# Three matmuls of 256 columns in place of a pair, in a kernel with split float32 weights

## The chip, the core and the metric

The kernel runs on one core of a Trainium2 chip. The metric is the device time of one execution in microseconds, from the runs of the kernel alone; the profile is one further execution, recorded with every engine's instructions. The engines are called by the profile's short names: PE is TensorE (PEld its loading of weights), DVE is VectorE, ACT is ScalarE, POOL is GpSimd, SP is SyncE, whose queue issues the loads.

## The reference

One layer of a decoder trunk on 256 positions and 2048 channels, in float32:

```python
h = rms_norm(x, pre_g)
proj = h @ w_in
a_u, a_v, a_g, b_x, b_g, x_q, x_g, gate_logits = jnp.split(proj, splits, axis=-1)
y_a = spatial_gating(a_u, a_v, sg_ln_g, sg_ln_b, sg_w, sg_b) * jax.nn.silu(a_g)
y_b = s5_branch(b_x, ..., glu_w, glu_b) * jax.nn.silu(b_g)
y_x = memory_cross_attention(x_q, rms_norm(mem, mem_g), xa_wk, xa_wv) * jax.nn.silu(x_g)
branch = jnp.einsum('bsnc,ncd->bsnd', jnp.stack([y_a, y_b, y_x], axis=2), w_branch)
gates = jax.nn.sigmoid(gate_logits.reshape(bsz, seq, N_BRANCH, D_MODEL))
out = jnp.sum(gates * branch, axis=2) @ w_out
return x + rms_norm(out, post_g)
```

Each of a_u to x_g is 1024 channels wide, the gate logits 3 x 2048. The state-space branch (s5_branch) runs a complex scan over the positions for 64 groups of 16 channels, applies a GELU, and ends in a gated linear unit: y times the sigmoid of y @ glu_w + glu_b. The cross-attention has 4 heads over 256 memory tokens.

## The kernel before

**Split numbers.** Every large product is made of numbers split in two: the high part is the value rounded to the matmul's reduced format (float32r), the low part is the rest. A product is then high by high, high by low and low by high. The weights come from memory as float32 in pieces of 128 x 2048 (`load`), and each half piece is split by `split` (lines 86 to 94): ScalarE makes the high part (line 93), VectorE subtracts to get the low part (line 94), into one of three buffers of the tag "hl". The activations are split once: x into the 16 tiles `xhl`, the memory tokens into `mhl`, the state-space output into `ygl`.

**Two kinds of product.** In the time-major kind (`tm_mm`, lines 181 to 184) the activations are the loaded operand and the weights move, 512 columns at a time. The change doesn't touch it. In the channel-major kind the weights are loaded, 128 x 128 at a time, and the activations move: the result has 128 channels in the partitions and 256 positions (T) in the columns. Its step, for one block of 128 inputs, is `cm_mm` (lines 169 to 174): a pair of matmuls. One has the high weights and moves 512 columns, high and low activations side by side, into a result of two halves of 256 columns; the other has the low weights, moves the 256 high columns, and adds to the first half. The two halves are then added, which gives the three products. In every step but the first of a block the matmul with the low weights comes first (line 171); in the first it comes second (line 174). `cm_mm3` (lines 176 to 179) does the same in three matmuls of 256 columns into the first half alone; only wk uses it.

**Adding the halves.** `fold` (lines 230 to 234) copies the second half out of the accumulator with ScalarE (line 232) and adds the first half with VectorE (line 233) into a tile of the tag "w0". `fold_u` (lines 338 to 340) does the same into its destination, for u and for the queries. After `fold` come: a multiplication by `rx2`, the row of inverse norms (line 327), then a SiLU for w_ag and w_bg (`silu`, lines 692 to 696); the multiplication alone for w_xg (`evac_xg`, line 755) and w_au (line 874); a sigmoid with bias for the GLU (line 908).

**Order.** `cm_block` runs a block of 16 steps, 8 for each half piece; `cm_pairs` runs two blocks into one accumulator of two banks (of which there are two), then calls the function that takes the result out. The stages that matter here, in order: the first four blocks of w_bx together with the splitting of x; four more blocks of w_bx; w_xq (8 blocks); wk (8, three matmuls); wv (time-major); w_xg (8); the gates and w_br of the attention (time-major); w_av (time-major); w_ag and w_au (8 each); gates and w_br again; w_bg (8); gates; the GLU (8 blocks of 8 steps); w_br, w_out (time-major).

The order of the instructions on PE is the order of the program. On the other engines it is fixed when the program is built, by priorities, with the splits of weights put ahead (line 88). Between half blocks `pump` (lines 188 to 208) lets background work run by a credit of estimated microseconds: above all the state-space branch (`s5_main`), whose elementwise work and scans sit on VectorE, and the small steps of attention, layer norm and spatial gating. Loads go through SyncE's queue, three pieces ahead.

Of the kernel before, what the change touches and what calls it, by code (L numbers as in the profile page):

```python
# [9 lines left out]
F32 = mybir.dt.float32  # L10
# [3 lines left out]
AF = mybir.ActivationFunctionType  # L14
ALU = mybir.AluOpType
# [3 lines left out]
P = 128  # L19
D = 2048  # L20
T = 256
# [23 lines left out]
def trunk(ctx: ExitStack, tc: tile.TileContext, I, out):  # L45
    nc = tc.nc
    v, a, g, pe = nc.vector, nc.scalar, nc.gpsimd, nc.tensor
# [18 lines left out]
    def nm(s):  # L66
        n_[0] += 1
        return f"{s}_{n_[0]}"
# [8 lines left out]
    def load(src):  # L77
        t = rawp.tile([P, 2048], F32, tag="raw", name=nm("raw"))
        nc.sync.dma_start(out=t, in_=src)
        return t  # L80
# [86 lines left out]
                                   in1=hi.bitcast(F32), op0=ALU.mult, op1=ALU.subtract)  # L167

    def cm_mm(ps, wh, wl, hl, first, last):
        if not first:  # L170
            pe.matmul(ps[:, 0:T], lhsT=wl, rhs=hl.moving(0), start=False, stop=False)  # L171
        pe.matmul(ps, lhsT=wh, rhs=hl.moving_both(), start=first, stop=last)  # L172
        if first:
            pe.matmul(ps[:, 0:T], lhsT=wl, rhs=hl.moving(0), start=False, stop=False)

    def cm_mm3(ps, wh, wl, hl, first, last):
        pe.matmul(ps[:, 0:T], lhsT=wh, rhs=hl.moving(0), start=first, stop=False)
        pe.matmul(ps[:, 0:T], lhsT=wh, rhs=hl.moving(1), start=False, stop=False)
        pe.matmul(ps[:, 0:T], lhsT=wl, rhs=hl.moving(0), start=False, stop=last)
# [29 lines left out]

    rate = {"cm": 0.62, "tm": RT[6]}  # L210

    def cm_block(ps, raw, hl, mm_=cm_mm):
        for hf in range(2):
            wh, wl = split(raw[:, hf * 1024:(hf + 1) * 1024], CM_OFF)
            for k in range(8):
                kk = hf * 8 + k
                mm_(ps, wh[:, k * P:(k + 1) * P], wl[:, k * P:(k + 1) * P], hl[kk], kk == 0, kk == 15)
            pump(rate["cm"])

    def tm_quarter(acc, raw, hl, kq, nk):  # L220
# [6 lines left out]
                    tm_mm(acc[tb], wh[:, sl], wl[:, sl], hl[kk], tb, kk == 0, kk == nk - 1)  # L227
            pump(rate["tm"])

    def fold(ps, bc):  # L230
        t = wk.tile([P, 2, T], F32, tag="w0", name=nm("f"))
        a.copy(out=t, in_=ps[:, :, T:2 * T])
        v.tensor_tensor(out=t, in0=ps[:, :, 0:T], in1=t, op=ALU.add)
        return t

    def cm_pairs(src, nblk, hl, evac, mm_=cm_mm):
        for bp in range(nblk // 2):
            ps = acc_tile()
            for b in range(2):
                cm_block(ps[:, b], load(src[2 * bp + b]), hl, mm_)  # L240
            evac(bp, ps)

    wz = wk.tile([P, 512], BF16, tag="w1", name="wz", padded_shape=[P, 1024])
# [82 lines left out]
    def mul_to(dst, t, bc):  # L326
        v.tensor_tensor(out=dst, in0=t, in1=bc, op=ALU.mult)
# [7 lines left out]
        with tc.high_priority(offset=AHEAD):  # L335
            norm_split(r, g_mem, mhl[hf * 8:hf * 8 + 8], hf * 8)

    def fold_u(d, ps):
        a.copy(out=d, in_=ps[..., T:2 * T])
        v.tensor_tensor(out=d, in0=ps[..., 0:T], in1=d, op=ALU.add)  # L340

    b45 = [bup.tile([P, 512], F32, tag="bu", name=f"bx{i}") for i in (4, 5)]
    cm_block(b45[0], load(I["w_bx"][0]), xhl)
    for i in range(2):
        fold_u(u[:, 2 * i:2 * i + 2, :], acc0[i])
    cm_block(b45[1], load(I["w_bx"][1]), xhl)
    ps = acc_tile()
    cm_block(ps[:, 0], load(I["w_bx"][2]), xhl)
    for i in range(2):
        fold_u(u[:, 4 + i, :], b45[i])  # L350
    nc.sync.dma_start(out=sp, in_=I["s5p"])
    for i in range(2):
        nc.sync.dma_start(out=Cin[i], in_=I["s5c"][:, i])
    cm_block(ps[:, 1], load(I["w_bx"][3]), xhl)
    fold_u(u[:, 6:8, :], ps)
    cbt = s5c.tile([P, NQ, 2, 32], F32, tag="cb", name="cb")
    g.memset(cbt, 0.0)
    NB = 16
# [293 lines left out]
    ssx, ssm = [], []  # L652

    def evac_q(bp, ps):
        fold_u(qT[:, 2 * bp:2 * bp + 2, :], ps)
        if bp < 2:
            mem_half(bp)
        else:
            ssx.append(rms_sq(I["x"][bp - 2]))
        if bp == 3:  # L660
            bg[2].append(rms_row("x", ssx, ((u, "u"), (qT, "q"))))
# [21 lines left out]
                a.activation(out=dst[:, tb, n * 512:(n + 1) * 512], in_=acc[:, tb], func=AF.Copy,  # L683
                             scale=nrm[key][0][:, tb:tb + 1])

    cm_pairs(I["wk"], 8, mhl, evac_k, cm_mm3)
    tm_rows(I["wv"], mhl, vv, "m")
    rstd_x, rx2 = nrm["x"]

    sx = slot("H0", [P, 8, T])  # L690

    def silu(ps, d):
        mul_to(d, fold(ps, rx2), rx2)
        t = wk.tile([P, 2, T], F32, tag="w0", name=nm("sl"))
        a.activation(out=t, in_=d, func=AF.Sigmoid)
        v.tensor_tensor(out=d, in0=d, in1=t, op=ALU.mult)
# [55 lines left out]
        yield 1.2  # L752

    def evac_xg(bp, ps):
        mul_to(sx[:, 2 * bp:2 * bp + 2, :], fold(ps, rx2), rx2)

    rate["cm"] = RT[2]
    bg[2].extend(attn(h) for h in range(4))
# [111 lines left out]
    yA += [slot("H3", [P, 4, 2, T], F32R), slot("X0", [P, 4, 2, T], F32R)]  # L870

    def evac_au(bp, ps):
        t = fold(ps, rx2)
        mul_to(t, t, rx2)
        d = zT[:, 2 * bp:2 * bp + 2, :]
        v.tensor_tensor(out=d, in0=d, in1=t, op=ALU.mult)
        bg[2].append(sg_z(bp))
# [21 lines left out]
    for bp in range(4):  # L899
        ps = acc_tile()  # L900
        raw = load(I["glu"][bp])
        for b in range(2):
            wh, wl = split(raw[:, b * 1024:(b + 1) * 1024], CM_OFF)
            for k in range(8):
                cm_mm(ps[:, b], wh[:, k * P:(k + 1) * P], wl[:, k * P:(k + 1) * P], ygl[k], k == 0, k == 7)
        t = fold(ps, None)
        for i in range(2):
            a.activation(out=t[:, i, :], in_=t[:, i, :], func=AF.Sigmoid, bias=glu_b[:, 2 * bp + i:2 * bp + i + 1])
        b = slice(2 * bp, 2 * bp + 2)
        v.tensor_tensor(out=t, in0=t, in1=u[:, b, :], op=ALU.mult)  # L910
        v.tensor_tensor(out=t, in0=t, in1=sb[:, b, :], op=ALU.mult)
        for i in range(2):
            d = yB[2 * bp + i]
            split_to(d[:, 0], d[:, 1], t[:, i])
# [210 lines left out]
```

## Time and profile before

| | |
|---|---|
| runs of the kernel | 935.72, 937.12, 935.7 us; median 935.72 us |
| the profiled execution | 934.47 us, its span 932.7 us |
| granted TensorE clock, mean | 0.998 of full speed |
| VectorE, line 94, 319 splits of 128 x 1024 | 388.7 us, 1220 ns each |
| ScalarE, line 93, 319 of them | 331.5 us, 1044 ns each |
| DMA, mean | 207 GB/s |

The span runs from the first to the last instruction of the program. A row of the table of windows gives, for a stretch of it, the length and then the busy time and the number of instructions of each engine, the granted clock, the busy share of the DMA engines and their rate. A row of instructions gives line, engine, operation, what is written from what, the size and number; then the busy time in microseconds and the mean of one in nanoseconds; then the idle time of the engine just before them and what ended it. A row of a timeline begins with start and duration in microseconds. Matmuls overlap: a matmul's duration in the profile (380 ns for 512 columns) is longer than the distance to the next one's start, so it is the starts that tell the pace.

### The profile page before, as it was taken

How to read it: one execution, taken by the hardware profiler on the slowest of the kernel's cores; microseconds unless marked ns; L12 is line 12 of the kernel's file. 1: busy time of each engine (PE TensorE's matmuls, PEld its weight loads, DVE VectorE, ACT ScalarE, POOL GpSimd, SP SyncE). 2: the span in 40 equal slices, each digit the busy share in tenths (PEclk: the TensorE clock that was granted, in tenths of full speed). 3: DMA queues.
4: the chain of work that ended last, by engine and by line, in shares of the span. 5: the costliest groups of instructions: out<-in, count | busy, mean ns of one | idle time of the engine just before them, and what ended most of it. 6: DMA issues, size and time to landing. Idle time of an engine off the chain costs nothing.

```text
span 932.7 us, 13296 instructions
## 1 busy us (share of the span) xinstructions
PE 912.2 (98%) x4992; PEld 801.5 (86%) x4992; DVE 785.0 (84%) x1382; ACT 544.9 (58%) x896; POOL 22.1 (2%) x46
## 2 busy tenths in 40 slices
PE   9999999989999999999999999999999999999996
PEld 7988998889888888788999888878887888998896
DVE  7899759965779999999887799999998977876565
ACT  7656756655557656565544576655665646644452
POOL 1000000000000000000000000000000000000000
PEclk9999999999999999999999999999999999999999
DMA  9767765545355565655655545555556456657652
GB/s 360 285 238 279 285 213 182 198 160 220 136 201 177 197 226 202 221 192 181 231 182 192 214 158 199 201 187 208 184 188 223 165 210 228 217 181 272 217 188 91
DMA packets 30465, 193.35 MB, mean 207 GB/s; under 512 B 3904, under 2 KB 4416, under 8 KB 8640
## 3 DMA queue, kind: packets, MB, share of 16 engines
q1 hardware_dynamic: 28288, 186.18, 55.7%
q0 software_dynamic: 1536, 4.20, 1.3%
q10 hardware_dynamic: 576, 2.12, 0.6%
q8 instruction: 39, 0.64, 0.3%
q14 instruction: 26, 0.21, 0.1%
HBM read 190.39 MB, written 2.10 MB: 206 GB/s over the span
## 4 chain that ended last, share of the span: by engine, by line
PE 49%; DVE 37%; ACT 7%; issue 5%; DMA 1%; DVEq 0%; POOL 0%; ACTq 0%; POOLq 0%
DVE hl L94 15%; PE acc L172 11%; PE acc L183 9%; PE acc L184 9%; PE acc L182 9%; DVE p L368 7%; PE acc L171 5%; DVE p L598 4%; ACT hl L93 3%; DVE E L371 2%; DVE s L368 1%; DVE B L528 1%; PE po L738 1%; ACT U L531 1%; DMA raw<-mem 1%
## 5 line engine op out<-in xcount | busy, mean ns | idle before, releaser
L94 DVE TENSOR_TENSOR hl<-raw,hl 128x1024 fp32r<-128x1024 f32 x319 | 388.7, 1220 | 108.7 <-ACT hl L93 105.8
L93 ACT CAST hl<-raw 128x1024 fp32r<-128x1024 f32 x319 | 331.5, 1044 | 193.6 <-PE acc L184 101.1
L172 PE MATMUL acc<-x,hl 128*128 128x512 f32 x736 | 242.7, 384 | 0.0
L171 PE MATMUL acc<-x,hl 128*128 128x256 f32 x690 | 190.5, 276 | 2.4 <-DVE hl L94 2.4
L183 PE MATMUL acc<-hl,x 128*128 128x512 f32 x448 | 172.4, 385 | 3.9 <-DVE hl L94 3.4
L182 PE MATMUL acc<-hl,x 128*128 128x512 f32 x448 | 171.4, 383 | 0.0
L184 PE MATMUL acc<-hl,x 128*128 128x512 f32 x448 | 169.9, 379 | 0.0
L172 PEld LDWEIGHTS acc<-x,hl 128*128 128x128 f32 x736 | 137.5, 190 | 17.7 <-ACT hl L93 0.7
L171 PEld LDWEIGHTS acc<-x,hl 128*128 128x128 f32 x690 | 132.3, 192 | 6.3 <-DVE hl L94 5.0
L183 PEld LDWEIGHTS acc<-hl,x 128*128 128x128 f32 x448 | 84.8, 189 | 22.6 <-DVE hl L94 11.7
L182 PEld LDWEIGHTS acc<-hl,x 128*128 128x128 f32 x448 | 84.9, 190 | 13.2 <-issue 2.1
L184 PEld LDWEIGHTS acc<-hl,x 128*128 128x128 f32 x448 | 84.8, 189 | 11.1
L183 PE MATMUL acc<-hl,H 128*128 128x512 f32 (+1 forms) x224 | 84.2, 376 | 1.1 <-DVE hl L94 1.1
L182 PE MATMUL acc<-hl,H 128*128 128x512 f32 (+1 forms) x224 | 83.6, 373 | 0.0
L184 PE MATMUL acc<-hl,H 128*128 128x512 f32 (+1 forms) x224 | 83.3, 372 | 0.0
L545 ACT ACTIVATE t<-E,pwr 128x32 f32<-128x32 f32 (+2 forms) x96 | 33.9, 354 | 33.2 <-DVE E L371 32.1
L183 PEld LDWEIGHTS acc<-hl,H 128*128 128x128 f32 x224 | 42.4, 189 | 8.9 <-DVE hl L94 3.6
L182 PEld LDWEIGHTS acc<-hl,H 128*128 128x128 f32 x224 | 42.5, 190 | 5.6 <-issue 0.4
L184 PEld LDWEIGHTS acc<-hl,H 128*128 128x128 f32 x224 | 42.5, 190 | 5.2
L368 DVE TENSOR_TENSOR p<-p,E 128x512 f32<-128x512 f32 x64 | 44.0, 687 | 0.8
L598 DVE TENSOR_TENSOR_SCAN p<-s5r,p 128x256 f32<-128x256 f32 x64 | 43.1, 696 | 0.8
L368 DVE TENSOR_TENSOR p<-bu,E 128x512 f32<-128x512 f32 x64 | 41.8, 685 | 2.0 <-PE bu L557 2.0
(248 smaller groups left out, 1270.4 us busy)
## 6 DMA issues: line engine op xcount, KB each, us to landing
raw<-w_gate SPq DMA_DIRECT2D x48, 1024.0 KB, 4.7
raw<-w_br SPq DMA_DIRECT2D x24, 1024.0 KB, 4.7
raw<-w_out SPq DMA_DIRECT2D x16, 1024.0 KB, 4.8
raw<-w_xq SPq DMA_DIRECT2D x8, 1024.0 KB, 4.8
raw<-wk SPq DMA_DIRECT2D x8, 1024.0 KB, 4.8
raw<-wv SPq DMA_DIRECT2D x8, 1024.0 KB, 4.7
raw<-w_xg SPq DMA_DIRECT2D x8, 1024.0 KB, 4.8
raw<-w_av SPq DMA_DIRECT2D x8, 1024.0 KB, 4.8
```

Of the source, the lines that this page charges most:

```text
L93: a.copy(out=hi, in_=src)
L94: v.tensor_tensor(out=lo, in0=src, in1=hi.bitcast(F32), op=ALU.subtract)
L171: pe.matmul(ps[:, 0:T], lhsT=wl, rhs=hl.moving(0), start=False, stop=False)
L172: pe.matmul(ps, lhsT=wh, rhs=hl.moving_both(), start=first, stop=last)
L182: pe.matmul(ps, lhsT=hl.stationary(0, tb), rhs=two(wh), start=first, stop=False)
L183: pe.matmul(ps, lhsT=hl.stationary(0, tb), rhs=two(wl), start=False, stop=False)
L184: pe.matmul(ps, lhsT=hl.stationary(1, tb), rhs=two(wh), start=False, stop=last)
L368: v.tensor_tensor(out=o, in0=i0, in1=i1, op=op)
L371: v.scalar_tensor_tensor(out=o, in0=i0, scalar=s, in1=i1, op0=o0, op1=o1)
L528: v.tensor_tensor(out=B4[64:P], in0=rw[64:P], in1=B4[64:P].bitcast(F32), op=ALU.subtract)
L545: a.activation(out=t, in_=E[:, :, lo_], func=AF.Copy, scale=ci)
L598: v.tensor_tensor_scan(out=p2[:, ri], data0=rb, data1=p1[:, ri], initial=0.0, op0=ALU.mult, op1=ALU.add)
```

## The change

All channel-major products take the three matmuls of 256 columns. `cm_mm` gets the body of `cm_mm3`, which goes; so do the parameter `mm_`, `fold`, and the adds of `fold_u`, which becomes `evac_u`, a copy by ScalarE. The multiplications by rx2 and the GLU's sigmoid read the first half of the accumulator directly.

```diff
     def cm_mm(ps, wh, wl, hl, first, last):
-        if not first:
-            pe.matmul(ps[:, 0:T], lhsT=wl, rhs=hl.moving(0), start=False, stop=False)
-        pe.matmul(ps, lhsT=wh, rhs=hl.moving_both(), start=first, stop=last)
-        if first:
-            pe.matmul(ps[:, 0:T], lhsT=wl, rhs=hl.moving(0), start=False, stop=False)
-
-    def cm_mm3(ps, wh, wl, hl, first, last):
         pe.matmul(ps[:, 0:T], lhsT=wh, rhs=hl.moving(0), start=first, stop=False)
         pe.matmul(ps[:, 0:T], lhsT=wh, rhs=hl.moving(1), start=False, stop=False)
         pe.matmul(ps[:, 0:T], lhsT=wl, rhs=hl.moving(0), start=False, stop=last)
...
-    def fold(ps, bc):
-        t = wk.tile([P, 2, T], F32, tag="w0", name=nm("f"))
-        a.copy(out=t, in_=ps[:, :, T:2 * T])
-        v.tensor_tensor(out=t, in0=ps[:, :, 0:T], in1=t, op=ALU.add)
-        return t
...
-    def fold_u(d, ps):
-        a.copy(out=d, in_=ps[..., T:2 * T])
-        v.tensor_tensor(out=d, in0=ps[..., 0:T], in1=d, op=ALU.add)
+    def evac_u(d, ps):
+        a.copy(out=d, in_=ps[..., 0:T])
...
     def silu(ps, d):
-        mul_to(d, fold(ps, rx2), rx2)
+        mul_to(d, ps[:, :, 0:T], rx2)
...
     def evac_xg(bp, ps):
-        mul_to(sx[:, 2 * bp:2 * bp + 2, :], fold(ps, rx2), rx2)
+        mul_to(sx[:, 2 * bp:2 * bp + 2, :], ps[:, :, 0:T], rx2)
...
     def evac_au(bp, ps):
-        t = fold(ps, rx2)
-        mul_to(t, t, rx2)
+        t = wk.tile([P, 2, T], F32, tag="w0", name=nm("f"))
+        mul_to(t, ps[:, :, 0:T], rx2)
...
-        t = fold(ps, None)
+        t = wk.tile([P, 2, T], F32, tag="w0", name=nm("f"))
         for i in range(2):
-            a.activation(out=t[:, i, :], in_=t[:, i, :], func=AF.Sigmoid, bias=glu_b[:, 2 * bp + i:2 * bp + i + 1])
+            a.activation(out=t[:, i, :], in_=ps[:, i, 0:T], func=AF.Sigmoid, bias=glu_b[:, 2 * bp + i:2 * bp + i + 1])
```

More of the change, by code (lines that the diff above doesn't have):

```diff
@@ L210, in trunk, with cm_block @@
     rate = {"cm": 0.62, "tm": RT[6]}
-    def cm_block(ps, raw, hl, mm_=cm_mm):
+    def cm_block(ps, raw, hl):
         for hf in range(2):
@@ L216, in cm_block @@
                 kk = hf * 8 + k
-                mm_(ps, wh[:, k * P:(k + 1) * P], wl[:, k * P:(k + 1) * P], hl[kk], kk == 0, kk == 15)
+                cm_mm(ps, wh[:, k * P:(k + 1) * P], wl[:, k * P:(k + 1) * P], hl[kk], kk == 0, kk == 15)
             pump(rate["cm"])
@@ L228, in tm_quarter, with cm_pairs @@
             pump(rate["tm"])
-    def fold(ps, bc):
-        t = wk.tile([P, 2, T], F32, tag="w0", name=nm("f"))
-        a.copy(out=t, in_=ps[:, :, T:2 * T])
-        v.tensor_tensor(out=t, in0=ps[:, :, 0:T], in1=t, op=ALU.add)
-        return t
-    def cm_pairs(src, nblk, hl, evac, mm_=cm_mm):
+    def cm_pairs(src, nblk, hl, evac):
         for bp in range(nblk // 2):
@@ L239, in cm_pairs @@
             for b in range(2):
-                cm_block(ps[:, b], load(src[2 * bp + b]), hl, mm_)
+                cm_block(ps[:, b], load(src[2 * bp + b]), hl)
             evac(bp, ps)
@@ L344, in trunk @@
     for i in range(2):
-        fold_u(u[:, 2 * i:2 * i + 2, :], acc0[i])
+        evac_u(u[:, 2 * i:2 * i + 2, :], acc0[i])
     cm_block(b45[1], load(I["w_bx"][1]), xhl)
@@ L349, in trunk @@
     for i in range(2):
-        fold_u(u[:, 4 + i, :], b45[i])
+        evac_u(u[:, 4 + i, :], b45[i])
     nc.sync.dma_start(out=sp, in_=I["s5p"])
@@ L354, in trunk @@
     cm_block(ps[:, 1], load(I["w_bx"][3]), xhl)
-    fold_u(u[:, 6:8, :], ps)
+    evac_u(u[:, 6:8, :], ps)
     cbt = s5c.tile([P, NQ, 2, 32], F32, tag="cb", name="cb")
@@ L654, in evac_q @@
     def evac_q(bp, ps):
-        fold_u(qT[:, 2 * bp:2 * bp + 2, :], ps)
+        evac_u(qT[:, 2 * bp:2 * bp + 2, :], ps)
         if bp < 2:
@@ L684, in tm_rows @@
                              scale=nrm[key][0][:, tb:tb + 1])
-    cm_pairs(I["wk"], 8, mhl, evac_k, cm_mm3)
+    cm_pairs(I["wk"], 8, mhl, evac_k)
     tm_rows(I["wv"], mhl, vv, "m")
```

## The prediction, made before the change was run

> **What bounds the kernel now.** First the page: the share of the span in which each engine is busy.
>
> ```profile
> span 932.7 us, 13296 instructions
> ...
> PE 912.2 (98%) x4992; PEld 801.5 (86%) x4992; DVE 785.0 (84%) x1382; ACT 544.9 (58%) x896; POOL 22.1 (2%) x46
> ```
>
> PE, the matmuls, is busy nearly always; PEld, the loading of weights, comes next. An average can hide a stage with another limit, so the second view is the table of windows, cut at the start of the first matmul of each stage that concerns us. In order: w_xq, wk (which already uses three matmuls), w_xg, w_ag with w_au, w_bg, the GLU; then two stretches without a wait, two blocks of w_bx in pairs and 47 steps of wk in threes.
>
> ```profile
> core 0: us, PE busy (x) PEld busy (x) DVE busy (x) ACT busy (x) POOL busy (x), PEclk, DMA share, GB/s
> 48.05:92.44 44.39, 43.02 (x258) 38.21 (x257) 43.20 (x139) 26.18 (x43) 1.06 (x2) 1.00 0.68 252
> 92.44:136.75 44.31, 43.85 (x389) 43.47 (x388) 30.37 (x52) 27.69 (x42) 0.20 (x1) 1.00 0.69 253
> 180.49:233.89 53.40, 50.94 (x306) 46.84 (x304) 35.74 (x60) 31.94 (x55) 0.54 (x1) 1.00 0.52 192
> 417.20:505.64 88.44, 87.86 (x539) 79.91 (x538) 77.94 (x134) 45.94 (x62) 0.54 (x1) 1.00 0.55 200
> 640.13:685.80 45.67, 44.86 (x277) 39.27 (x276) 43.08 (x72) 27.83 (x49) 1.07 (x2) 1.00 0.55 202
> 774.10:796.06 21.96, 21.49 (x129) 19.36 (x128) 16.59 (x22) 15.58 (x25) 0.00 (x0) 1.00 0.60 217
> 27.09:37.57 10.48, 10.48 (x66) 9.65 (x64) 8.88 (x27) 5.08 (x7) 0.00 (x0) 1.00 0.71 262
> 104.46:120.21 15.75, 15.75 (x144) 15.75 (x143) 13.32 (x30) 11.92 (x20) 0.10 (x1) 1.00 0.69 261
> ```
>
> TensorE is granted the full clock in all of them (the column with 1.00) and is the bound in all of them. VectorE comes close in two: 43.20 of 44.39 us in w_xq, 43.08 of 45.67 in w_bg; in w_xg it has 35.74 of 53.40. So a nanosecond more on TensorE counts in full, and a nanosecond less on VectorE counts only where a matmul waits for it. The third view, the list of waits by window, says where that is.
>
> ```profile
> PE acc L171 <- DVE hl L94: 1.4, 3, 0.7
> ...
> PE acc L171 <- DVE hl L94: 0.5, 2, 0.3
> ...
> PE acc L171 <- DVE hl L94: 0.5, 1, 0.5
> PE acc L174 <- DVE hl L94: 0.3, 1, 0.3
> ...
> PE acc L183 <- DVE hl L94: 4.4, 9, 1.7
> PE tp L728 <- DVE p L722: 2.5, 1, 2.5
> ...
> PE acc L171 <- ACT H L93: 0.4, 1, 0.4
> ```
>
> Each row gives the total in us, the times and the longest. The first is w_xq, the second w_ag with w_au, the next two are w_bg; the last three come from the list of the whole span: line 183 belongs to the stages with activations as weights, which don't change, the transposes of line 728 to w_xg, the last row to the GLU. The first four are one kind: the first matmul of a half block needs the low part of the weights, which VectorE subtracts at line 94, and it is late. The rows understate the loss, because matmuls overlap; the timeline of the first one shows by how much.
>
> ```profile
> 66.28 0.27 PE L171 MATMUL acc<-x,hl 128*128 128x256 f32 x1
> 66.39 0.38 PE L172 MATMUL acc<-x,hl 128*128 128x512 f32 x1
> 67.26 0.38 PE L171 MATMUL acc<-x,hl 128*128 128x256 f32 x1 [0.48 <-DVE hl L94]
> 67.47 0.38 PE L172 MATMUL acc<-x,hl 128*128 128x512 f32 x1
> ```
>
> From start to start a 256 takes 0.11 and a 512 takes 0.33 - 0.11 = 0.22 (a pair is 327.5 ns, below). Here the 512 takes 0.87 and the next 256 takes 0.21: 0.65 + 0.10 = 0.75 us lost where the row names 0.48. I add 0.27 to each such wait.
>
> **The change part by part.** *A. The third matmul (cost).* How many steps there are:
>
> ```profile
> L172 PE MATMUL acc<-x,hl 128*128 128x512 f32 x736 | 242.7, 384 | 0.0
> ```
>
> By the code there are 48 blocks of 16 steps and 8 of the GLU with 8: 832. The row has 736 of them; the 2 x 16 into the tiles bx and the 64 of the GLU have other names. 832 steps of a 512 and a 256 become three 256s; the columns streamed, 768, stay. The price is in the table: the stretch from 27.09 holds two blocks of 16 steps, 10.48 / 32 = 327.5 ns a pair; the stretch from 104.46 lies between the starts of 48 triples, 15.75 / 47 = 335.1 ns a triple (its x144 are 47 triples and three matmuls across its ends). Its PEld is busy for all 15.75 us against 9.65 of 10.48 with pairs: the loads have become as long as the matmuls. 7.6 ns x 832 = **+6.3 us**. Bounds: wk moves data of another tile (mhl, not xhl) in the same form; if each 256 took what one takes behind a 512 in the timeline (0.11, so 0.33 for three), the step would cost 2.5 ns more, 2.1 us in all; by the whole stage of wk, its waits and other matmuls included (44.31 / 128 = 346 ns), 18.7 ns more, 15.5 us. I take the stretch of triples without a wait, which is the operation itself.
>
> Here a rule of the Trainium skill speaks otherwise. The page "TensorE: Matmul & The Clock Gate", section "Back-to-back issue gap", gives N / 2.4 + 2.5 ns for a matmul of N columns: by it a triple would be 328 ns and a pair 325, one fixed cost of 2.5 ns more, an estimate of 2.1 us for 832 steps. The trace agrees for the pair to 1% and not for the triple, 335.1 measured, so the measured row goes into the sum.
>
> *B. The adds (relief of VectorE).*
>
> ```profile
> L233 DVE TENSOR_TENSOR f<-acc,f 128x512 f32<-128x512 f32 x20 | 13.7, 683 | 0.0
> ...
> L327 DVE TENSOR_TENSOR H<-f,bc_x 128x512 f32<-128x512 f32 x8 | 5.5, 690 | 0.2
> ...
> L340 DVE TENSOR_TENSOR X<-acc,X x4: 677/684/684, 64.0 to 97.5; 128x512 f32<-128x512 f32 x4
> L340 DVE TENSOR_TENSOR U<-acc,U x3: 684/692/692, 27.3 to 52.6; 128x512 f32<-128x512 f32 x3
> L340 DVE TENSOR_TENSOR U<-bx,U x2: 416/418/421, 35.1 to 40.9; 128x256 f32<-128x256 f32 x2
> ```
>
> VectorE loses 13.7 us at line 233 and 4 x 0.68 + 3 x 0.69 + 2 x 0.42 = 5.6 at line 340, 19.3 us of adds: four of 0.68 each in w_xq, w_xg, w_ag, w_au, w_bg and the GLU, the rest for u. The multiplication by rx2 (690 ns out of SBUF) now reads PSUM, as the add did in 683 ns: no change of price. ScalarE loses the 20 copies of line 232, counted at nothing, since by the table it is at most 71% busy (15.58 of 21.96 us in the GLU); line 339 keeps its copies, and the GLU's sigmoid keeps its size and reads PSUM. VectorE's add of line 233 had an idle time of 0.0 before it, so it never waited for the copy; the multiplication in its place waits for the last matmul alone and can start earlier. Behind it in VectorE's queue stand the next splits, and behind those a half block of matmuls; that it comes up too early is as unlikely as the add's 0.0 says. No DMA is added or moved. An accumulator is free after one reader instead of two; there is no row of PE waiting for one, so that gains nothing.
>
> Only where a split of line 94 is late does this relief turn into time. In w_xq VectorE runs almost without a gap, so an add removed moves all later splits forward:
>
> ```profile
> 63.97 0.68 DVE L340 TENSOR_TENSOR X<-acc,X 128x512 f32<-128x512 f32 x1
> ...
> 66.00 1.21 DVE L94 TENSOR_TENSOR hl<-raw,hl 128x1024 fp32r<-128x1024 f32 x1
> ```
>
> The split at 66.00 is the one that the matmul of 67.26 waited for, and such an add stands 2 us ahead of it.
>
> *C. The order of the three.* In the pair the low weights come first in every step but the first; in the triple the two matmuls with the high weights, which ScalarE makes before VectorE starts, come first. A late split is met 2 x 0.112 = 0.22 us later. For the first step of a block (line 174) the cover was one 512, 0.22 us, so nothing changes there.
>
> *D. What B and C save.* w_xq: 1.4 + 3 x 0.27 = 2.2 lost in three waits, each under 0.9; add and order together take away about that much for each, and the stage as a whole bears it out: VectorE would have 43.20 - 4 x 0.68 = 40.5 us to do in 44.39 - 2.2 + 128 x 0.0076 = 43.2, so what is left there is TensorE itself. Saved 2.1. w_ag with w_au: 0.5 + 2 x 0.27 = 1.0; saved 0.9, since order alone covers 0.22 of each. w_bg: 0.5 + 0.3 + 2 x 0.27 = 1.3 and some near misses; the row of line 174 stands at the stage's start and stays; saved 1.0. w_xg and the GLU: the waits are for p of the attention and for ScalarE, neither behind an add; saved 0. Together **-4.0 us**. If all of it and as much again as the near misses of w_bg fell away, some 5.5 (an estimate); if only the order helped, in six waits at most, 6 x 0.22 = 1.3.
>
> *E. The sum.* 6.3 - 4.0 = **+2.3 us**. The profiled execution took 934.47 us, 1.8 around its span of 932.7; the median of the three runs is 935.72, 1.25 higher. On the median: 935.7 + 2.3 = **938.0 us**. With the ends of D alone it would run from +0.8 to +5.0, with those of A added from -3.4 to +14.2.
>
> **The rivals.**
> 1. *The waits stay* (slower). VectorE's instructions stand in an order fixed when the program is built; when an add goes, background work of the state-space branch can move up into its place, and the split is as late as before. For it: w_xq is 97% busy on VectorE with such work. Against it: that work is finite within a stage, and 40.5 us fit. Only C saves, at most 1.3: +5.0, **940.7 us**. It decides as soon as less than half of D comes true.
> 2. *The third matmul is cheap* (faster). It would cost as a lone 256 does, 0.11: +2.1 - 4.0 = -1.9, **933.8 us**. For it: that row. Against it: 47 triples in a row at 335.1. This is the result that the page's rule gives.
> 3. *The relief reaches further* (faster). The transposes of line 728 wait 2.5 us once, and line 183 waits 4.4 us in nine places for the same splits. If the first went (2.5 + 0.27) and a third of the others (a third of 4.4 + 9 x 0.27 = 6.8, so 2.3), +2.3 - 5.1 = -2.8, **932.9 us**. Against it: there are no adds of halves in the stages of line 183, nor in w_xg before that wait, so only a new order of VectorE could do it.
> 4. *The change doesn't do what it says*: the second matmul with the same weights might need no load, and the triple be cheaper yet.
>
> ```profile
> L178 PEld LDWEIGHTS acc<-H,hl 128*128 128x128 f32 x128 | 24.6, 192 | 0.0
> ```
>
> Line 178 loads its weights 128 times for 128 matmuls, so no.
>
> **How the numbers follow.** A measurement of this kernel can tell about 0.2%, 1.9 us, from no change. My forecast, +2.3, has 0.53, and with its own range from +0.8 to +4.0 it lies partly within the 1.9 (0.20) and partly beyond (0.33). Rival 1 has 0.20, all slower. Rival 2 has 0.07, at the edge of faster, and rival 3 has 0.13, mostly beyond it: 0.15 faster, 0.05 within. Rival 4 has 0. Another order with new waits, beyond rival 1's price, has 0.07. Faster 0.15, same 0.25, slower 0.60. The range takes in rivals 1 and 2 at their prices and what lies around them, from 933.4 to 941.4; left out are most of rival 3, the new waits, and the far ends of A, 0.2 in all.
>
> **What would show it.** In the profile afterwards: some 832 matmuls more, all 256 wide, from start to start 0.112, and PEld near 100% in the stages named (A); no adds of halves, VectorE at some 766 us (B); w_xq at about 43.2 us, w_ag with w_au at 88.44 + 1.9 - 0.9 = 89.5, w_bg at 45.6, w_xg at 53.40 + 1.0 = 54.4 (D). The prediction is wrong if a triple isn't 335 ns with xhl, if the waits of line 94 stay in w_xq and w_bg, or if the transposes' wait of 2.5 us changes.

## The result, and the profile after

The changed kernel takes 941.96 us (median; 940.66 to 945.53) beside 935.92 us for the kernel before: a ratio of 1.0065 [1.0052, 1.0078], **6.1 us slower**, 0.6 us above the range. The profiled execution took 940.84 us with a span of 939.0, against 934.47 and 932.7. One execution of a kernel further down, g3, took 4996 us and is left out of every figure. The page of the profile after, first the span and the engines, then three groups of matmuls (busy us, mean ns; then the idle time before them):

```profile
span 939.0 us, 14908 instructions
...
PE 918.7 (98%) x5824; PEld 831.5 (89%) x5824; DVE 769.3 (82%) x1353; ACT 535.9 (57%) x876; POOL 22.7 (2%) x46
...
L172 PE MATMUL acc<-x,hl 128*128 128x256 f32 x736 | 204.2, 277 | 2.9 <-DVE hl L94 2.4
L170 PE MATMUL acc<-x,hl 128*128 128x256 f32 x736 | 204.1, 277 | 0.1
L171 PE MATMUL acc<-x,hl 128*128 128x256 f32 x736 | 202.4, 275 | 0.0
```

There are 832 matmuls more (5824 against 4992), and all of the channel-major kind are 256 wide. VectorE has 15.7 us less to do (785.0 to 769.3). Yet the matmul that needs the low weights, line 172 now, waits as before, when it was line 171:

```profile
L171 PE MATMUL acc<-x,hl 128*128 128x256 f32 x690 | 190.5, 276 | 2.4 <-DVE hl L94 2.4
```

The table of windows of the kernel after, in order: four blocks of w_bx, w_xq, wk, w_xg, w_ag with w_au, w_bg, the gates behind it, the GLU:

```profile
core 0: us, PE busy (x) PEld busy (x) DVE busy (x) ACT busy (x) POOL busy (x), PEclk, DMA share, GB/s
...
27.87:49.30 21.43, 21.43 (x194) 21.43 (x193) 18.80 (x82) 12.66 (x22) 2.20 (x4) 1.00 0.80 299
49.32:95.31 45.99, 44.47 (x387) 43.32 (x385) 42.15 (x127) 28.83 (x49) 1.08 (x2) 1.00 0.64 232
95.31:141.25 45.94, 44.94 (x390) 43.84 (x389) 27.68 (x43) 25.75 (x36) 0.20 (x1) 1.00 0.65 237
...
185.04:239.28 54.24, 52.02 (x434) 51.21 (x432) 34.06 (x57) 30.62 (x52) 0.54 (x1) 1.00 0.53 189
422.62:512.74 90.12, 89.95 (x795) 89.03 (x794) 74.26 (x127) 42.61 (x55) 0.54 (x1) 1.00 0.56 196
647.28:693.40 46.12, 45.34 (x405) 44.06 (x404) 43.60 (x74) 26.84 (x48) 1.07 (x2) 1.00 0.58 205
693.40:779.89 86.49, 86.49 (x428) 74.30 (x427) 74.54 (x121) 49.42 (x79) 0.54 (x1) 1.00 0.58 202
779.89:802.28 22.39, 21.97 (x193) 21.58 (x192) 16.10 (x21) 14.48 (x24) 0.00 (x0) 1.00 0.61 213
```

Two windows of the kernel before that the prediction didn't need, the four blocks of w_bx and the gates behind w_bg:

```profile
27.09:48.05 20.96, 20.96 (x130) 19.29 (x128) 19.32 (x71) 13.23 (x22) 1.59 (x4) 1.00 0.76 272
685.80:774.10 88.30, 87.53 (x427) 73.85 (x426) 77.64 (x127) 49.75 (x81) 0.54 (x1) 1.00 0.56 200
```

From these windows, stage by stage in us. "Price" is the prediction's 7.6 ns for each step of the stage; "left" is what the change of the stage leaves when the price is taken off, so a saving is negative there. Stages not listed differ by 0.05 at most, and the stretch ahead of the first matmul is 0.2 shorter.

```
stage              before   after   change   price    left
start (64 steps)    22.29   23.30    +1.01    0.49   +0.52
w_bx (64)           20.96   21.44    +0.48    0.49   -0.01
w_xq (128)          44.39   45.99    +1.60    0.97   +0.63
wk (0)              44.32   45.95    +1.63    0      +1.63
w_xg (128)          53.40   54.24    +0.84    0.97   -0.13
w_ag, w_au (256)    88.44   90.12    +1.68    1.95   -0.27
w_bg (128)          45.67   46.13    +0.46    0.97   -0.51
gates behind w_bg   88.30   86.49    -1.81    0      -1.81
GLU (64)            21.96   22.39    +0.43    0.49   -0.06
span               932.7   939.0     +6.3     6.3     0.0
```

The price came as forecast, and the last column adds up to nothing where the prediction had -4.0. Savings are there, 1.8 us of them in a stage that the change doesn't touch; new losses of the same size stand in wk, which the change doesn't touch either, in w_xq and at the start. Each profile is one execution: the start takes 22.1 to 22.5 us in the profiles of the kernel before and of two kernels below that leave the start alone (e4, h1), so its +0.5 is the least certain of them.

### The profile page after: what moved, and what is told of

Read it like the earlier page. It is cut to its first block, busy times and chain, and to the rows that moved or that the text cites. A ratio compares the mean times of both kernels' runs of the same rounds, so it can differ in the third digit from the quotient of the medians.

```text
span 939.0 us, 14908 instructions
## 1 busy us (share of the span) xinstructions
PE 918.7 (98%) x5824; PEld 831.5 (89%) x5824; DVE 769.3 (82%) x1353; ACT 535.9 (57%) x876; POOL 22.7 (2%) x46
## 4 chain that ended last, share of the span: by engine, by line
PE 56%; DVE 31%; ACT 5%; issue 5%; DMA 3%; SPq 0%; DVEq 0%; ACTq 0%
DVE hl L94 12%; PE acc L176 10%; PE acc L177 10%; PE acc L175 10%; PE acc L172 7%; PE acc L171 7%; PE acc L170 7%; DVE p L354 6%; DVE p L584 3%; ACT hl L93 3%; DVE E L357 2%; DMA raw<-mem 1%; DVE s L354 1%; DMA raw<-x 1%; DVE B L514 1%
## 5 line engine op out<-in xcount | busy, mean ns | idle before, releaser
L172 PE MATMUL acc<-x,hl 128*128 128x256 f32 x736 | 204.2, 277 | 2.9 <-DVE hl L94 2.4
L170 PE MATMUL acc<-x,hl 128*128 128x256 f32 x736 | 204.1, 277 | 0.1
L171 PE MATMUL acc<-x,hl 128*128 128x256 f32 x736 | 202.4, 275 | 0.0
L172 PEld LDWEIGHTS acc<-x,hl 128*128 128x128 f32 x736 | 141.2, 192 | 6.1 <-DVE hl L94 6.1
L170 PEld LDWEIGHTS acc<-x,hl 128*128 128x128 f32 x736 | 141.4, 192 | 1.3 <-ACT hl L93 0.8
L171 PEld LDWEIGHTS acc<-x,hl 128*128 128x128 f32 x736 | 141.4, 192 | 0.2
L175 PEld LDWEIGHTS acc<-hl,x 128*128 128x128 f32 x448 | 84.7, 189 | 13.3 <-issue 2.1
L172 PE MATMUL acc<-H,hl 128*128 128x256 f32 x192 | 53.4, 278 | 1.0 <-DVE hl L94 0.9
L170 PE MATMUL acc<-H,hl 128*128 128x256 f32 x192 | 53.1, 276 | 0.3 <-ACT H L93 0.3
L171 PE MATMUL acc<-H,hl 128*128 128x256 f32 x192 | 52.9, 276 | 0.1
L176 PEld LDWEIGHTS acc<-hl,H 128*128 128x128 f32 x224 | 42.4, 189 | 9.1 <-DVE hl L94 3.6
```

The source lines that it names most:

```text
L175: pe.matmul(ps, lhsT=hl.stationary(0, tb), rhs=two(wh), start=first, stop=False)
L176: pe.matmul(ps, lhsT=hl.stationary(0, tb), rhs=two(wl), start=False, stop=False)
```

## The experiments

The theory at this point: the price is real, and the savings were given back because the order of VectorE and ScalarE was made anew when the program was built without the adds. The rivals: (a) the triple costs more than 335 ns in some stages; (b) taking the adds away saves nothing, in whatever order; (c) it is the high-first order of the matmuls that loses.

**What each edit does alone.** Three with the adds kept (the low-activation product goes to the second half, as in the pair); the pair without the adds; the pair with the high weights always first:

```diff
 # e1_three_with_adds, in cm_mm; fold and the adds stay
+        pe.matmul(ps[:, 0:T], lhsT=wh, rhs=hl.moving(0), start=first, stop=False)
+        pe.matmul(ps[:, T:2 * T], lhsT=wh, rhs=hl.moving(1), start=False, stop=False)
+        pe.matmul(ps[:, 0:T], lhsT=wl, rhs=hl.moving(0), start=False, stop=last)
 # e2_pair_no_adds: the changed kernel, but cm_mm is the pair of before; wk keeps its three
 # e3_pair_high_first, in cm_mm
+        pe.matmul(ps, lhsT=wh, rhs=hl.moving_both(), start=first, stop=False)
+        pe.matmul(ps[:, 0:T], lhsT=wl, rhs=hl.moving(0), start=False, stop=last)
```

> Three matmuls of 256 in place of the pair, but the product of high weights and low activations still goes into the second half, and the halves are still added. So the price of the third matmul without the relief of VectorE. Theory (the price is 7.6 ns a step, and what the change was to win back on VectorE wasn't won because the background work moves up into the gaps): 6.3 us of pace, less at most 1.3 for the order of the matmuls, so +5 to +6.5 against before, about as slow as the changed kernel. Rival (the price is real but the relief did work, and something else that came with reading PSUM directly was lost): clearly slower than the changed kernel, +8 to +10. Rival (the matmuls are cheap and the loss is all in waits that the missing adds shifted): near 0 to +2.

> The pair as before (wk keeps its three), but the evacuations of the changed kernel: the second half is never read, so the product of high weights and low activations is left out. The relief of VectorE alone, without the price. Theory (the order of VectorE's work is remade and the relief is taken up by background work): -1.5 to +1 against before. Rival (the prediction's step D): -4.0. In the trace the waits for line 94 in w_xq and wk tell which: 2.2 us before in w_xq.

> The pair and the adds as before, but the matmul with the high weights comes first in every step, so a late low half is met 0.22 us later. Step C alone. If the order of the matmuls saves its share of the six waits: up to -1.3; if VectorE's order is remade by so small a change and its waits fall elsewhere: anything from -2 to +2 with other waits than before. The pace of a pair stays at 327.5 ns.

Measured: e1 1.0078 [1.0064, 1.0092], +7.3 us; e2 0.9966 [0.9955, 0.9976], -3.3 us; e3 0.9989 [0.9979, 0.9999], -0.9 us. So taking the adds away is worth some 3 us in e2, against rival (b), though e2's order was made anew too; the -1.5 to +1 that the theory had expected of e2 is missed. High first loses nothing, against (c). But the three matmuls with the adds cost 7.3, more than their price of 6.3 less anything that high first gains; e1 loses 2.6 us in wk (46.92 against 44.32), where not one matmul or add was edited. Something that no edit names costs 2 us in e1 (7.3 - 6.3 + 0.9) and 4 in the changed kernel (6.1 - 6.3 + 3.3 + 0.9).

**Why a triple takes 335 ns.** In w_xg alone the step is made of four matmuls, of 256, 256, 128 and 128 columns; the columns together stay 768.

```diff
 # e4_four_in_xg, for w_xg alone
+        pe.matmul(ps[:, 0:T], lhsT=wh, rhs=hl.moving(0), start=first, stop=False)
+        pe.matmul(ps[:, T:2 * T], lhsT=wh, rhs=hl.moving(1), start=False, stop=False)
+        for c in range(2):
+            pe.matmul(ps[:, c * P:(c + 1) * P], lhsT=wl, rhs=hl.moving(0)[:, c * 64:(c + 1) * 64], start=False, stop=last and c == 1)
```

> As before, but in w_xg alone each step is four matmuls: the pair's 512 columns in two of 256, the 256 columns of the low weights in two of 128; 768 columns as ever, four loads of weights. If a load of weights sets a floor of 111.7 ns for each matmul: 4 x 111.7 = 447 ns a step, 119 more than the pair, 15.3 us for 128 steps. If the price is a fixed cost for each matmul on top of its columns (2.5 ns to 4 ns each): 333 to 340 ns a step, 1 to 1.5 us in all.

One execution: 947.86 us; w_xg takes 66.36 us against 53.40, 12.96 more. PE's wait before the first transposes of w_xg, 2.46 us in the kernel before, is gone there, so the steps cost 15.4, as the floor of the expectation has it. The timeline of PE in w_xg of this run (start, duration; x2 is two matmuls in one row), then that of its loads:

```profile
199.82 0.33 PE L182 MATMUL acc<-x,hl 128*128 128x256 f32 x1
199.99 0.28 PE L183 MATMUL acc<-x,hl 128*128 128x256 f32 x1
200.10 0.33 PE L185 MATMUL acc<-x,hl 128*128 128x128 f32 x2
200.27 0.33 PE L182 MATMUL acc<-x,hl 128*128 128x256 f32 x1
```

```profile
199.88 0.19 PEld L183 LDWEIGHTS acc<-x,hl 128*128 128x128 f32 x1
199.99 0.30 PEld L185 LDWEIGHTS acc<-x,hl 128*128 128x128 f32 x2
200.21 0.19 PEld L182 LDWEIGHTS acc<-x,hl 128*128 128x128 f32 x1
```

A step lasts from 199.82 to 200.27, 0.45 us for the same 768 columns; over the stage the four gaps from start to start have medians of 165, 112, 58 and 112 ns, together 447 = 4 x 111.7. The triple is 3 x 111.7 = 335. The matmuls start at uneven distances, the loads every 0.11 us. So it is the number of matmuls that each load their own weights that sets the time here, not the columns. Two loads, 223 ns, are well below the 327.5 ns that a pair takes for its 768 columns; three, 335 ns, are the first to outlast the columns. The Trainium skill, page "TensorE: Matmul & The Clock Gate", section "LDWEIGHTS (loading the stationary operand)", gives P / 1.2 ns for a load of P columns, 107 ns here; three of them would be 320 (an estimate), and the measured limit of 111.7 is 5% above it. Rival (a) falls as well: w_bx has 64 steps and no wait before or after, and went from 20.96 to 21.44 us, 7.5 ns a step; and in every stage of the kernel after the median from one start to the next of a triple is 112 ns.

**The order held.** VectorE and ScalarE each run their instructions in the order in which the built program has them. The next kernels force the order of the kernel before on both, the fallen instructions left out of the list. This orders instructions within an engine and adds no wait.

```diff
 # at the end of the program; ORDER is the order of the kernel before
+    no_sync = mybir.DependencyInfo(mybir.DependencyClass.NoSync, mybir.DependencyReason.DATA)
+    for eng, order in ORDER.items():
+        mine = [i for i in list(nc.cur_bb.bb.instructions) if i.engine == getattr(mybir.EngineType, eng)]
...
+        for p_, q_ in zip(order, order[1:]):
+            tc.add_manual_dep(mine[q_], mine[p_].name, no_sync, reason="order")
```

f1 is the changed kernel so held, f2 is e2, f3 is e1. f4 is e3, with wk in pairs and four adds as well.

> The changed kernel, with VectorE's and ScalarE's instructions held in the order of the kernel before (the adds and copies that fell away left out of it). Theory (the pace costs 6.3, and the relief of VectorE is worth some 4 us when the order stays, but the order remade at build time took it back): +2 to +3 against before, 3 to 4 us under the changed kernel; w_xq without most of its waits, wk at 44.3 to 44.5 us as before instead of 45.95, the stretch before the GLU near 88 instead of 86.5. Rival (the relief is worth little in any order, step D was wrong in itself): +5 to +6.5, like the changed kernel.

> The pair without the adds (the product of high weights and low activations is left out, as in e2), in the order of before. The relief alone with nothing else moved. Theory: -3 to -4.5 against before, all of it out of the waits for line 94 in w_xq, w_ag and w_bg. Rival (the relief is worth little): -1.5 to 0.

> Three matmuls and the adds kept (as in e1), in the order of before. The price of the third matmul alone: 832 steps less the 64 where the start waits for loads anyway, 5.8 to 6.3, less up to 1.3 for the matmuls with high weights coming first and less what a slower TensorE waits less: +4 to +6 against before. If it stays at the +7.3 of e1, the order that the builder made isn't what e1 lost beyond the pace.

> The other way round: wk takes the pair and four adds too, every pair has the high weights first, and the order is that of before (the four new adds find their own place). wk is 128 steps: 128 x 7.6 ns = 1.0 us off; the order of the matmuls saves up to 1.3. Theory: -1.0 to -2.3 against before. Rival (the adds in wk make splits late there, VectorE has 30.4 of 44.3 us): -1 to +0.5.

Measured: f1 1.0004 [0.9995, 1.0013], +0.4 us; f2 0.9972 [0.9961, 0.9983], -2.6; f3 1.0043 [1.0028, 1.0057], +4.0; f4 0.9998 [0.9989, 1.0008], -0.2. **The changed kernel in the old order costs nothing that these ratios can tell: 6.1 - 0.4 = 5.7 us of it were the order** (4.5 when executions of like granted clock are compared, as the last section does). For three with adds the order cost 7.3 - 4.0 = 3.3; for pairs it cost nothing (-3.3 free, -2.6 held). A remade order isn't bad as such: here it came out bad in both kernels with triples, and not in e2. Held, the parts can be read: the third matmul with the high weights first costs 4.0 (f3), 2.3 under the price, and taking the adds away brings 3.6 more (f3 to f1). What of the 2.3 is the order of the three, and what comes of a slower TensorE that waits less for its splits, no run separates; with pairs high first brought 0.9 (e3). f4 was to win 1.0 to 2.3 and won nothing that can be told: in its profile wk is 0.65 us shorter, but the gates behind w_bg are 0.28 longer and the stretch behind the GLU 0.82.

The list of waits of PE over the whole span, before (line 179 is wk's), after and f1 (one line more in f1's kernel ahead of it, so its line 173 is line 172 of after):

```profile
PE acc L171 <- DVE hl L94: 2.4, 6, 0.7
...
PE acc L179 <- DVE hl L94: 0.5, 2, 0.3
```

```profile
PE acc L176 <- DVE hl L94: 3.7, 7, 1.7
PE acc L172 <- DVE hl L94: 3.3, 10, 0.8
```

```profile
PE acc L177 <- DVE hl L95: 3.6, 7, 1.5
...
PE acc L173 <- DVE hl L95: 1.2, 4, 0.4
```

After, line 172 is the low weights' matmul of every channel-major step, so it stands against three lines of before: 171, 179 and 174 (0.3 in one place, in the prediction), 3.2 us in 9 places. After it is 3.3 in 10: the waits for late splits didn't shrink, although 19.3 us of adds were gone. In the old order they are 1.2 in 4. The other kind, line 176, is the same after and in f1.

**Which engine, and where.** g2 holds only VectorE, g3 only ScalarE. In g1 and k1 the order is free but for one thing: the squares of the rows of x and mem (line 272 after, 285 before), whose sums go into the norms. Only ScalarE needs the loaded rows for them, and their loads wait in the same queue as those of the weights. A row is squared in two halves. In the order of before, from the second row on, both halves stand behind a copy that takes a result out; in the remade one the first half stands ahead of that copy.

```diff
 # g1: behind the copy of its own pair of blocks; k1: in place, behind the copy of the pair before it
+            with tc.issue_after(after):
+                a.activation(out=rr, in_=rr, func=AF.Square, accum_out=ss[:, hf:hf + 1])
```

> The changed kernel, with one thing held on ScalarE: the squares of the rows of x and mem (line 272) are issued only behind the copy that takes the pair's result out, as in the kernel before, instead of ahead of a split while their load is still on its way. The rest of the order is free. If ScalarE's standing at these squares is what w_xq and wk lost: wk back from 45.95 to some 44.4 us, w_xq down by up to 1, +3.5 to +4.5 against before. If it is VectorE's order: +6, like the changed kernel.

> The changed kernel with VectorE alone in the order of before; ScalarE's order is free. With f1 (both held, +0.4): if VectorE's order is the cause, near +0.5 to +1.5; if ScalarE's is, +4 to +6.

> The changed kernel with ScalarE alone in the order of before; VectorE's order is free. The counterpart of g2: if ScalarE's order is the cause, near +0.5 to +1.5; if VectorE's is, +4 to +6; if both have a share, g2 and g3 both lie between.

> The changed kernel, with the squares of line 272 issued behind the copy of the pair before theirs, the place that they have in the kernel before; all else on ScalarE and VectorE free. In g1 they were put a whole pair later, so their buffers came back late and the loads of wk waited (10.0 us of ScalarE's time); here they don't. If their place is what ScalarE's order costs: wk from 45.95 to 43.5 to 44.5 us, ScalarE's waits for the rows of mem from 9.0 to under 3, and +1 to +3 against before, near g3 (+1.4). If it is some other part of ScalarE's order (the steps of the state-space branch among the splits): +5 to +6.5, like the changed kernel.

Measured: g1 1.0078 [1.0064, 1.0092], +7.3; g2 1.0056 [1.0042, 1.0071], +5.2; g3 1.0015 [1.0005, 1.0025], +1.4; k1 1.0030 [1.0019, 1.0040], +2.7. With ScalarE's order held, 6.1 - 1.4 = 4.7 us come back, and the squares alone are 6.1 - 2.7 = 3.4 us of it (2.2 among executions of like clock; between the two profiles wk alone is 2.6 shorter). So it is above all ScalarE's order. ScalarE's list of waits, the row of the squares of mem, before, after and in k1:

```profile
ACT raw L285 <- DMA raw<-mem: 1.6, 1, 1.6
```

```profile
ACT raw L272 <- DMA raw<-mem: 9.0, 2, 5.2
```

```profile
ACT raw L275 <- DMA raw<-mem: 2.0, 2, 1.2
```

How a wait of ScalarE, which is 57% busy, reaches PE can be followed in wk of the kernel after, on ScalarE, then VectorE, then PE (the bracket names the idle time before the row and what ended it):

```profile
110.10 1.06 ACT L272 ACTIVATE raw<-raw 128x1024 f32<-128x1024 f32 x1 [5.18 <-DMA raw<-mem]
...
111.16 1.03 ACT L93 CAST hl<-raw 128x1024 fp32r<-128x1024 f32 x1
112.10 0.58 ACT L657 COPY M<-acc 128x512 f32<-128x512 f32 x1
```

```profile
112.22 1.22 DVE L94 TENSOR_TENSOR hl<-raw,hl 128x1024 fp32r<-128x1024 f32 x1 [6.04 <-ACT hl L93]
```

```profile
112.46 0.28 PE L171 MATMUL acc<-H,hl 128*128 128x256 f32 x1
113.50 0.38 PE L172 MATMUL acc<-H,hl 128*128 128x256 f32 x1 [0.77 <-DVE hl L94]
```

ScalarE stands 5.18 us at the squares for a load that hasn't come, the next high part stands behind it, VectorE stands 6.04 us for that, and PE loses 113.50 - 112.46 - 0.11 = 0.93 us. ScalarE comes to these squares at 104.9, 9.6 us into wk, and the copy of the stage's first result stands behind them. In the kernel before it comes to them at 105.8, 13.3 us into wk, when that copy is done, and waits 1.65; the load itself is no later than it was (these squares start as it lands, 14.8 us into wk, before 15.0):

```profile
104.83 0.58 ACT L671 COPY M<-acc 128x512 f32<-128x512 f32 x1
...
107.41 1.07 ACT L285 ACTIVATE raw<-raw 128x1024 f32<-128x1024 f32 x1 [1.65 <-DMA raw<-mem]
```

The other two free kernels bear it out: in e1 the squares stand ahead of wk's first copy too and wait 5.5 us, and wk takes 46.92; in e2 they come behind it and wait 0.2, and wk takes 43.32. With the squares in place wk takes 43.33 us (k1), with no wait of PE left in it. g1 put them too late: wk is 44.71, w_xq 47.57, since the buffers of the rows come back late and loads of weights with them:

```profile
ACT hl L93 <- DMA raw<-wk: 10.0, 5, 3.9
```

g2 shows what a held order does when it meets a free one, so it doesn't price VectorE's order. Its wk takes 48.69 us against 43.93 in f1 (the other stages together are 2.1 longer in its profile), because VectorE stands for a small state-space step whose other operand ScalarE now makes later:

```profile
102.33 0.48 DVE L358 SCALAR_TENSOR_TENSOR E<-E,pwr,t 128x64 f32<-128x64 f32 x2 [4.43 <-ACT t L532]
```

PE waits 3.43 us for the split behind it, and then the granted clock is down for some 3 us:

```profile
105.00:106.00 1.00, 1.00 (x6) 1.00 (x6) 1.00 (x2) 0.00 (x0) 0.00 (x0) 0.50 0.09 33
```

**Left open.** k1 is still 2.3 us above f1. By stages, the start has 22.98 against 22.16, w_xq 46.08 against 44.54, w_ag with w_au 90.14 against 89.22, w_bg 46.13 against 45.10. The 0.9 of w_ag with w_au goes with VectorE's order: 90.1 to 90.5 in all five kernels with triples that leave it free (after, e1, g1, g3, k1), 89.2 to 89.6 in the three that hold it (f1, f3, g2). In w_xq and w_bg each engine's order has a share: about 45.45 with either one held, 45.99 with neither, 44.54 with both in w_xq; 45.40 (ScalarE held), 45.66 (VectorE), 46.13 and 45.10 in w_bg. In w_xq the rows tell a little more: the split that VectorE reaches latest starts 3.6 us after its high part is ready where VectorE's order is held (f1, g2) and 4.2 to 4.5 us after it where it is free (the kernel after, g3, k1). Beyond that no single instruction was found, and no run here separates them.

**Where three matmuls pay.** In w_bg the relief reaches into the next stage. So: the kernel before, in its order, with three matmuls and no adds in w_bg alone.

```diff
 # h1_three_in_bg_alone
+    cm_pairs(I["w_bg"], 8, ..., silu(ps, ..., False), cm_mm3)
+    # silu: fold(...) if halves else ps[:, :, 0:T]
```

> The kernel before, in its order, with three matmuls and no adds in w_bg alone, the one stage where the relief came out larger than the pace (w_bg and the gates behind it together 131.6 us in f1 against 134.0 before). Expected: -2.4, the other stages as before. If the gain there came from the stages before it (earlier relief carried along): -0.5 to +0.5.

Measured: 0.9964 [0.9951, 0.9977], 934.27 us, **3.4 us faster than before** by the ratio, and faster than the changed kernel. Windows of w_bg and the gates behind it:

```profile
640.07:685.21 45.14, 44.84 (x406) 43.94 (x404) 42.51 (x71) 26.30 (x46) 1.07 (x2) 1.00 0.59 209
685.21:771.70 86.49, 86.49 (x428) 74.29 (x427) 75.70 (x124) 49.90 (x80) 0.54 (x1) 1.00 0.58 202
```

w_bg is 45.14 (45.67 before) and the gates 86.49 (88.30): 0.53 + 1.81 = 2.3 us in the profile, as forecast, and at the upper end of the ratio's interval (-4.6 to -2.2 us). The last section shows why 2 us is nearer the truth than 3.4: a fall of the granted clock that comes and goes was in one of h1's five executions, and in 11 of the 14 of before beside them.

## Why the prediction was wrong, by its steps

**A, the price: right.** 7.5 ns a step in w_bx, where nothing waits, against 7.6 forecast; by stages without a new wait the same. PEld is busy for all of 21.43 us there. Of the two figures weighed, the row held and the estimate of 2.1 us fell; e4 shows why: each load of weights takes its 111.7 ns. The section "Back-to-back issue gap" of the page "TensorE: Matmul & The Clock Gate" of the Trainium skill, from which the prediction took that estimate, gives its formula for an isolated matmul only, and says that in a stream of loads and matmuls both set the pace, with which the 335 ns agree.

**B, the adds: right in size,** 769.3 us on VectorE against 766 forecast, 15.7 less. The groups show the 19.3 us of adds gone, the multiplications as long from PSUM as they were, and no other group changed by more than 0.4; the 3.6 us between are neighbours that overlap on VectorE, whose time the page counts once: added one by one, the instructions' durations fall by 19.6 us.

**C, high first: of the right sign, its size not settled.** The prediction had put 1.3 for it alone. With pairs it brought 0.9 (e3); with triples and the order held it and a slower TensorE that waits less bring 2.3 together (f3).

**D, the savings: this is the step that failed, as rival 1 said it could.** It put -4.0; the sum over the stages is 0.0. The failing sentence is the one against rival 1, "that work is finite within a stage, and 40.5 us fit". VectorE did 42.15 us in w_xq, not 40.5, although 2.7 us of adds were gone, while its time in wk fell from 30.37 to 27.68: work of the next stage had moved up (one split and six steps of the tables E of the state-space branch, 2.7 us by their rows). The splits came as late as before. The one that VectorE reaches latest in w_xq, its high part and itself, before and after:

```profile
66.81 1.04 ACT L93 CAST hl<-raw 128x1024 fp32r<-128x1024 f32 x1 [1.65 <-PE acc L172]
...
72.17 1.23 DVE L94 TENSOR_TENSOR hl<-raw,hl 128x1024 fp32r<-128x1024 f32 x1
```

```profile
69.16 1.05 ACT L93 CAST hl<-raw 128x1024 fp32r<-128x1024 f32 x1 [1.99 <-PE acc L172]
...
74.67 1.22 DVE L94 TENSOR_TENSOR hl<-raw,hl 128x1024 fp32r<-128x1024 f32 x1
```

It starts 4.32 us after its high part is ready before, and 4.46 after. And the prediction asked only what VectorE's queue would do. The larger part of the loss came by ScalarE, whose order was remade too; the prediction had counted its change at nothing because it is at most 71% busy, but an engine with time to spare still stops the next split when it stands at a load.

Nor is busy time a proof in the old order. In f1 VectorE has 40.96 us in w_xq, near the 40.5, and the stage is 44.54, not 43.2, with two waits left:

```profile
PE acc L173 <- DVE hl L95: 0.7, 2, 0.4
```

"What is left there is TensorE itself" was thus wrong in both orders. What the stage saved in f1 is 0.97 - 0.15 = 0.8 of the 2.1 forecast.

The other places, with the order held (f1), stage for stage against the forecast: w_ag with w_au saved 1.95 - 0.78 = 1.2 (0.9 forecast); w_bg 0.97 + 0.57 = 1.5 (1.0); the gates behind it 1.8 (0). The last one speaks against "so only a new order of VectorE could do it", said of rival 3: f1 and h1 have the old order and the same 1.8. VectorE ends w_bg with less work overdue and enters the gates ahead: without its four adds its 43.08 us of w_bg would be 40.4, it does 42.52 there, and some 2 us less in the gates. Its windows in f1, w_bg and the gates:

```profile
643.86:688.96 45.10, 44.80 (x406) 43.90 (x404) 42.52 (x71) 26.26 (x46) 1.07 (x2) 1.00 0.58 209
688.96:775.45 86.49, 86.49 (x428) 74.29 (x427) 75.67 (x124) 50.02 (x80) 0.54 (x1) 1.00 0.58 202
```

With 77.64 us of VectorE's work before, 75.67 in f1 and 74.54 after, the gates are free of PE's waits in both.

**E, the sum.** 6.3 - 4.0 = +2.3 was forecast; 6.3 - 0.0 = +6.3 came in the span. In the order of before it was +0.4 (f1), better than forecast. Rival 1 had the mechanism, but bounded its price by "Only C saves, at most 1.3", 5.0; the new order also made waits that were not there. Those "new waits, beyond rival 1's price" had a chance of 0.07. The transposes' wait, forecast unchanged, is 2.2 us where it was 2.5. w_xg was forecast at 54.4 and took 54.24.

## What to carry to other kernels

Where the order of the engines' instructions is made when the program is built, taking instructions out is two changes: their time, and a new order for the engines that the builder orders, which here cost 4.5 to 5.7 us of 936 with the same arithmetic; hold the old order to tell the two apart before judging the edit. A wide matmul cut in two costs nothing in columns, but each load of weights has a smallest time (111.7 ns for these), so look whether PEld is busy all the time in the stretch. And a relief of a nearly full engine can show in the stage behind the one where the work was taken away, which is also why three matmuls pay in w_bg and not everywhere. And look at the granted clock of each execution before a difference of 1 or 2 us is read as the edit's.

## What was not expected of the hardware

The granted clock falls after a wait of PE that in other executions leaves it alone. Before the transposes of w_xg PE waits 2.2 us both after and in f1. Windows around it in f1:

```profile
193.00:196.00 3.00, 0.78 (x7) 0.62 (x5) 2.06 (x6) 3.00 (x6) 0.00 (x0) 1.00 0.34 142
196.00:197.00 1.00, 1.00 (x8) 1.00 (x9) 1.00 (x1) 0.81 (x2) 0.00 (x0) 0.83 0.00 0
197.00:198.00 1.00, 1.00 (x6) 1.00 (x6) 1.00 (x3) 0.27 (x1) 0.00 (x0) 0.50 0.08 16
...
199.00:200.00 1.00, 1.00 (x7) 1.00 (x7) 0.00 (x0) 0.00 (x0) 0.00 (x0) 0.50 0.95 385
200.00:201.00 1.00, 1.00 (x9) 1.00 (x9) 0.00 (x0) 0.01 (x1) 0.00 (x0) 0.96 1.04 442
```

And in the kernel after:

```profile
198.00:202.00 4.00, 2.13 (x18) 2.16 (x19) 4.00 (x9) 3.10 (x6) 0.00 (x0) 1.00 0.05 18
202.00:206.00 4.00, 4.00 (x31) 3.84 (x30) 2.56 (x3) 1.04 (x1) 0.00 (x0) 1.00 0.71 262
```

In f1 the clock is at 0.50 for 3.4 us (3.0 from 197 to 200, 0.34 and 0.08 in the two windows beside), and w_xg takes 55.87 instead of 54.24 us. The profiles of seven kernels show it (e2, e3, f1, f2, g1, g2, g3: a mean of 0.81 to 0.86 over some 9 us of w_xg) and the others don't (1.00), with pairs as with triples.

The mean granted clock of an execution tells whether it had the fall: it is 0.994 to 0.996 in the seven profiles with it and 0.997 or 0.998 in the eight without. Of the kernel before, run again beside the experiments, 21 executions have 0.997 or more (median 935.41 us) and 50 have less (936.78). The shares differ from kernel to kernel, so a ratio of 1 or 2 us can hold this too. Against these two medians, executions of like clock (their number in brackets), in us:

```
kernel     by the ratio    0.997 or more    0.996 or less
changed        +6.1           +5.3 (2)         +5.3 (4)
f1             +0.4           +0.9 (5)         +0.6 (7)
f3             +4.0           +4.7 (4)         +4.2 (5)
g3             +1.4           +1.7 (5)         +1.9 (5)
k1             +2.7           +3.1 (4)         +3.1 (4)
e2             -3.3           -2.6 (6)         -2.5 (2)
h1             -3.4           -2.0 (4)         -2.2 (1)
```

No sign changes. The order's part becomes 4.5 us, the squares' 2.2, and h1's gain 2, near the 2.4 forecast. The Trainium skill, page "TensorE: Matmul & The Clock Gate", section "What's actually happening", says that the clock falls after an idle window of about 3.4 us and that the window runs free of the kernel; the fall's length, 3.4 us, agrees, and the second would fit that it comes in some executions; the first doesn't fit a wait of 2.2 us, with PE still 0.78 us busy between 193 and 196.
